# A hybrid diffusion block on one core: rotated queries' low part laid out over 128 rows, and another order of the two arms of the expert branch

## The chip, the cores and the metric

The kernel runs on one core of one Trainium2 chip. The metric is the time of one execution on the device in microseconds (us); the runs of a kernel are compared by their median. The engines are named as in the profile: PE is TensorE (PEld its weight loads), DVE is VectorE, ACT is ScalarE, POOL is GpSimd, and SP is SyncE, which issues the transfers of the weights. A letter q behind a name (PEldq, SPq) is the engine's sequencer.

## What is computed

Two layers act on 256 latent tokens and 256 context tokens of 1024 features. Each layer normalizes and modulates the tokens, projects them, runs three groups of heads side by side, projects back and adds; then comes a dense SwiGLU in layer 0 and a top-2-of-8 expert SwiGLU in layer 1, for latents only. Cut to what the change touches:

```python
qb = apply_rope(qb.reshape(b, n, 2 * DIFF_HEADS, HEAD_DIM), cos, sin)     # differential heads: rotated
na = neighbourhood_attention(qa, ka, va, ka_c, va_c, rpb)                 # neighbourhood heads: not rotated
s = einsum('bqhd,bkhd->bhqk', q, k) * HEAD_DIM ** -0.5                    # HEAD_DIM = 64
p = softmax(s); a = p[:, :, 0] - lam * p[:, :, 1]                         # two softmaxes per differential head
top_vals, top_idx = top_k(h @ w_router, 2)                                # how many latents an expert has depends on data
y = sum over e of gates[e] * (silu(h @ w1[e]) * (h @ w3[e])) @ w2[e]
```

## The kernel before

Tokens stay on chip with features on the partitions. Products are made in float32 from two parts each: a value is split into a rounded high part and the rest, its low part, and `mm3` (L222 to L224) adds high times high, high times low and low times high in one PSUM bank. Weights stream in through SP, are split on ACT (L100) and DVE (L101), and are used once.

**Attention.** A chunk of 128 columns of keys and of queries (`proj_kq`) makes one unit: two neighbourhood units ("na", 0 and 1; not rotated) and four differential ones ("df", 0 to 3; rotated by `rope`). A unit holds two heads or head parts m of 64 features, m = 0 in partitions 0 to 63 and m = 1 in 64 to 127. `key_parts` puts the keys' high part of m into its own half of the tile ks[m] and their low part into the other half; `query_parts` puts the queries' high part into both halves of qs[m], on ACT, and their low part into half m of one tile ql, on DVE (L536). So `scores` needs two products per m: qs[m] with ks[m] over all 128 rows (L560), which gives high times high and high times low, and ql with ks[m] over the 64 rows of half m (L563):

```python
for m in range(2):
    pe.matmul(s[m], qs[m][:, q], ks[m][:, :nk], start=True, stop=False, **kw)
for m in range(2):
    r = slice(64 * m, 64 * m + 64)
    pe.matmul(s[m], ql[r, q], ks[m][r, :nk], start=False, stop=True, **kw)
```

A unit has two query tiles in each group of tokens: layer 0 works on context and latents (256 and 512 keys), layer 1 on latents alone (512 keys). Per query tile the steps are scores, softmax (maximum and weighting on DVE, exponent on ACT), transposes on PE (L580), the split of the transposed block on ACT and DVE (L469, L471), and products with the values (`weigh`).

**Order of the work.** Attention steps wait in a queue with two lanes and are let out between projection products by `pace` (1.3 steps per call in layer 0, 0.4 in layer 1). `finish(keys)` lets out steps until the units named have none left. What order the instructions then get on each engine is decided by a scheduler. `proj_kq` calls finish for the units two before its own. The tiles of the neighbourhood's bias (`hparts["bias"]`, two buffers, loaded by `load_bias`, masked by `mask_bias`) are read when the neighbourhood's scores are finished (L566), and lie idle after that until the next layer.

**The experts.** `route` counts latents per expert and loads one number, few, into a register of every engine (L1300). `first_steps` runs the first part of expert 7, 32 latents wide, with weight tiles loaded ahead. Then `moe_main` branches (L1829): with few above 64 comes `moe_general`, a tree of further branches with a copy of `mix_experts` in each leaf; otherwise one `mix_experts` for two heavy experts and narrow ones for the others. In the program the general arm lies first, some 29,000 rows of PE's, and the arm for few latents behind it, directly ahead of the program's end. With these inputs the arm for few latents is the one that runs. Its weights are read into a ring of twenty tiles of 512 KB (`RAW_M`, L1194) and consumed by narrow products straight from the tile (L1619) and by wide ones after the split (L469, L471). `finish_out` ends the program: two output stores from SP and two from ACT (L1823), and then the engines meet (L1903).

Of the kernel before, what the change touches and what calls it, by code (L numbers as in the profile page):

```python
# [13 lines left out]
F32 = mybir.dt.float32  # L14
F32R = mybir.dt.float32r
# [114 lines left out]
def tile_hybrid_block(ctx: ExitStack, tc: tile.TileContext, x, c, cx, c_ctx, ada_w, ada_b, w_in, w_out, na_rpb,  # L130
                      diff_lambda, diff_subln, conv_w, ffn_w1, ffn_w3, ffn_w2, router_w, moe_w1, moe_w3, moe_w2,
                      final_gain, rope_cos, rope_sin, na_mask, out, dbg=None):
    nc = tc.nc
    sy, act, dve, pe, gp = nc.sync, nc.scalar, nc.vector, nc.tensor, nc.gpsimd
# [39 lines left out]
    hparts = {n: dstack["h"].enter_context(tc.tile_pool(name=n, bufs=1, side="right")) for n in ("hl", "hh", "bias")}  # L174
# [27 lines left out]
    def bank(tag, shape=(128, 512)):  # L202
        t = psum.tile([128, 512], F32, name=tag, tag=tag, bufs=4 if tag == "mm" else 2)
        n = int(np.prod(shape[1:]))
        v = t[:, :n]
        if len(shape) == 3:
            v = v.rearrange("p (a b) -> p a b", a=shape[1])
        return v
# [10 lines left out]
    def mm3(o, ah, al, bh, bl, start, stop):  # L219

        kw = dict(skip_group_check=True)
        return [pe.matmul(o, ah, bh, start=start, stop=False, **kw),  # L222
                pe.matmul(o, ah, bl, start=False, stop=False, **kw),  # L223
                pe.matmul(o, al, bh, start=False, stop=stop, **kw)]  # L224
# [19 lines left out]
    def step(n=1):  # L244
        for _ in range(n):
            for _ in range(2):
                i = turn[0]
                turn[0] ^= 1
                if lanes[i] is None and queue:
                    key, make = queue.popleft()  # L250
                    lanes[i] = key, make(i)
                if lanes[i] is not None:
                    if next(lanes[i][1], "end") == "end":
                        open_work[lanes[i][0]] -= 1
                        lanes[i] = None
                    break
# [3 lines left out]
    def pace():  # L260
        owed[0] += rate[0]
        step(int(owed[0]))
        owed[0] -= int(owed[0])
# [6 lines left out]
    def finish(*keys):  # L270
        while any(open_work.get(k, 0) for k in keys):
            step()
# [137 lines left out]
    st, mo = {}, {}  # L410

    def project(a, b, tags=("mm", "mm")):

        ps = [bank(t, (128, b - a)) for t in tags]
        for u in range(2):
            wh, wl = ws.next()
            wh = wh.rearrange("p (k n) -> p k n", k=4)
            wl = wl.rearrange("p (k n) -> p k n", k=4)
            for k in range(4):
                kt = 4 * u + k  # L420
                for i in range(2):
                    cs = slice(i * 128, (i + 1) * 128)
                    mm3(ps[i], wh[:, k, cs], wl[:, k, cs], hb["h"][:, kt, a:b], hb["l"][:, kt, a:b],
                        kt == 0, kt == KT - 1)
                pace()
        return ps
# [49 lines left out]
    def rope(src):  # L476

        ap = st["apool"]
        t = ap.tile([128, 256], F32, name="rope_t", tag="rope_t", bufs=2)
        u = ap.tile([128, 256], F32, name="rope_u", tag="rope_u", bufs=2)  # L480
        for o, i in ((0, 1), (1, 0), (2, 3), (3, 2)):
            dve.tensor_tensor(out=t[32 * o:32 * o + 32, :], in0=src[32 * i:32 * i + 32, :],
                              in1=sin_t[32 * i:32 * i + 32, :], op=ALU.mult)
        dve.tensor_tensor(out=u, in0=src, in1=cos_t, op=ALU.mult)
        dve.tensor_tensor(out=u, in0=u, in1=t, op=ALU.add)
        return u

    def proj_kq(l, name, rotate, ps=None):

        ap = st["apool"]  # L490
        q0 = 256 * l
        if ps is not None:
            pk, pq = ps
        elif l == 0:
            pk, pq = project(0, 512)
        else:
            ps = [bank("mm"), bank("mm", (128, 256))]
            for u in range(2):
                wh, wl = ws.next()
                wh = wh.rearrange("p (k n) -> p k n", k=4)  # L500
                wl = wl.rearrange("p (k n) -> p k n", k=4)
                for k in range(4):
                    kt = 4 * u + k
                    for i, a in ((0, 0), (1, 256)):
                        cs = slice(i * 128, (i + 1) * 128)
                        mm3(ps[i], wh[:, k, cs], wl[:, k, cs], hb["h"][:, kt, a:], hb["l"][:, kt, a:],
                            kt == 0, kt == KT - 1)
                    pace()
            pk, pq = ps
        units = [("na", 0), ("na", 1)] + [("df", j) for j in range(4)]  # L510
        finish(*units[:max(0, units.index(name) - 2)])

        ks = [ap.tile([128, 512], F32R, name="ks", tag="ks", bufs=6) for _ in range(2)]
        qs = [ap.tile([128, 512 - q0], F32R, name="qs", tag="qs", bufs=6) for _ in range(2)]
        ql = ap.tile([128, 512 - q0], F32R, name="ql", tag="ql", bufs=3)

        def rows_of(v):
            return v.rearrange("p (r n) -> p r n", n=GW)

        def key_parts(src, a):  # L520
            for m in range(2):
                r, o = slice(64 * m, 64 * m + 64), slice(64 - 64 * m, 128 - 64 * m)
                cs = slice(a, a + src.shape[1])
                act.activation(ks[m][r, cs], src[r], AF.Copy)
                dve.tensor_tensor(out=ks[m][o, cs], in0=src[r], in1=ks[m][r, cs].bitcast(F32), op=ALU.subtract)

        def query_parts(src, a):
            src, (hs, low) = rows_of(src), [[rows_of(q[:, a:a + src.shape[1]]) for q in qq] for qq in (qs, [ql])]
            if not rotate:

                src = src[:, :, ::-1]
            for m in range(2):
                r, o = slice(64 * m, 64 * m + 64), slice(64 - 64 * m, 128 - 64 * m)
                for h in (r, o):
                    act.activation(hs[m][h], src[r], AF.Copy, scale=0.125)
                dve.scalar_tensor_tensor(out=low[0][r], in0=src[r], scalar=0.125, in1=hs[m][r].bitcast(F32),  # L536
                                         op0=ALU.mult, op1=ALU.subtract)
        if rotate:
            uk = rope(pk[:, 256:512])
            key_parts(pk[:, :256], 0)  # L540
            uq = rope(pq[:, 256 - q0:512 - q0])
            if l == 0:
                query_parts(pq[:, :256], 0)
            key_parts(uk, 256)
            query_parts(uq, 256 - q0)
        else:
            key_parts(pk, 0)
            query_parts(pq, 0)
        st[name] = (ks, qs, ql)

    def scores(ln, kq, grp, qt, bias=None):

        ks, qs, ql = kq
        nk = 256 if grp == 0 else 512
        q0 = 256 * grp + 128 * qt - st["t0"]
        q = slice(q0, q0 + 128)
        s = [bank(f"at{ln}", (128, nk)) for _ in range(2)]
        kw = dict(skip_group_check=True)
        for m in range(2):
            pe.matmul(s[m], qs[m][:, q], ks[m][:, :nk], start=True, stop=False, **kw)  # L560
        for m in range(2):
            r = slice(64 * m, 64 * m + 64)
            pe.matmul(s[m], ql[r, q], ks[m][r, :nk], start=False, stop=True, **kw)  # L563
        if bias is not None:
            for m in range(2):
                dve.tensor_tensor(out=s[m][:, 256:], in0=s[m][:, 256:], in1=bias[m], op=ALU.add)  # L566
        return s
# [786 lines left out]
    def first_steps():  # L1354

        run = mo["run7"] = light((7,), 32)
        while len(mo["early"]) > TAIL:
            next(run)
            mo["run7_done"] = mo.get("run7_done", 0) + 1
        while mo["folds"]:  # L1360
            mo["folds"].popleft()()
        mo["run7_tasks"] = list(tasks)
        tasks.clear()
        mo["far"].close()
        mo["left"], mo["early"] = mo["early"], {}
# [460 lines left out]
    def moe_main():  # L1826
        route()
        first_steps()
        with tc.If(mo["few"] > 64) as more:  # L1829
            moe_general()  # L1830
        with more.Else():
            mix_experts([0, 1], [((7,), 32), ((2,), 64), ((3, 4, 5), 32)], begun=True)

    def moe_general():
# [18 lines left out]
        with first.Else():  # L1853
# [5 lines left out]
            with many.Else():  # L1859
                mix_experts([0, 1], [((7,), 64), ((2, 3), 64), ((4, 5), 64)])  # L1860

    do(lambda: None, moe_main)

    for add, _ in plan:
# [42 lines left out]
```

## Time and profile before

| what | before |
|---|---|
| median of 3 runs | 1706.23 us (1705.69 to 1714.27) |
| profiled execution | 1709.09 us, span 1707.3 us |
| mean granted PE clock | 0.986 |
| busy: PE, PEld, DVE, ACT, POOL | 96%, 74%, 60%, 37%, 1% |
| moved to and from HBM | 432 MB, 253 GB/s over the span |
| layer 0 attention and projections | about 60 to 265 us |
| layer 0 output and dense SwiGLU | about 265 to 715 us |
| layer 1 attention and projections | about 715 to 860 us |
| routing and first expert steps | about 860 to 914 us |
| the branch | 914 to 921 us |
| experts | 921 to 1695 us |
| final norm and stores | 1695 to 1707 us |

The span runs from the first to the last instruction of the program; 1.8 us of the execution lie around it. A busy PE is modelled, since matmuls overlap: what a matmul costs is better read from start to start in the timeline.

### The profile page before, as it was taken

The page shows a single profiled execution, that of the slowest core. Times are in us where ns is not written, and L with a number is a line of the kernel's source. Part 1 is how long each engine was busy: PE and PEld are TensorE (multiplying, and loading weights), DVE is VectorE, ACT ScalarE, POOL GpSimd, SP SyncE. Part 2 cuts the span into 40 slices and gives each one's busy share as a digit, 9 for nine tenths or more (in the row PEclk, how much of TensorE's full clock was granted, in tenths as well). Part 3 has the DMA queues.
Part 4 walks back from the last instruction along what each step waited for, and adds up shares of the span by engine and source line. Part 5 has one row for each costly group of instructions (what it writes and reads, how often), then busy time and mean ns, then how long its engine had stood idle before and what let it go on. Part 6 is the DMA issues. An engine that isn't in the chain of part 4 may idle for free. (4 is left out here: it accounts for less than half of the span.)

```text
span 1707.3 us, 28490 instructions
## 1 busy us (share of the span) xinstructions
PE 1639.5 (96%) x10942; PEld 1265.7 (74%) x10942; DVE 1030.1 (60%) x2043; ACT 639.0 (37%) x1057; POOL 17.6 (1%) x27
## 2 busy tenths in 40 slices
PE   7999999999999999999987999999999999999996
PEld 4777778988878888988772766676787686868773
DVE  4778877888877884788862353124454535354454
ACT  4555444422212232555533322222343234433341
POOL 0101000000000000000010000000000000000000
PEclk9999999999999999999988999999999999999999
DMA  9744343256555453352498999989999999999995
GB/s 287 179 132 111 99 149 99 88 185 197 197 169 171 154 185 111 99 149 75 162 355 312 409 380 340 349 332 401 360 368 398 364 353 364 405 386 350 388 381 193
DMA packets 234193, 434.66 MB, mean 255 GB/s; under 512 B 23496, under 2 KB 142784, under 8 KB 234048
## 3 DMA queue, kind: packets, MB, share of 16 engines
q1 hardware_dynamic: 232560, 432.14, 71.2%
q8 instruction: 88, 1.44, 0.3%
q10 hardware_dynamic: 1488, 0.62, 0.1%
q14 instruction: 57, 0.47, 0.1%
HBM read 431.66 MB, written 1.05 MB: 253 GB/s over the span
## 5 line engine op out<-in xcount | busy, mean ns | idle before, releaser
L471 DVE TENSOR_TENSOR wlo<-raw,whi 128x1024 fp32r<-128x1024 f32 x168 | 202.9, 1223 | 234.2 <-ACT whi L469 221.5
L222 PE MATMUL H<-xh,whi 128*128 128x256 f32 x896 | 257.2, 287 | 2.6 <-ACT whi L469 1.8
L224 PE MATMUL H<-xh,wlo 128*128 128x256 f32 x896 | 254.5, 284 | 2.0 <-DVE wlo L471 1.9
L223 PE MATMUL H<-xl,whi 128*128 128x256 f32 x896 | 254.1, 284 | 0.0
L469 ACT ACTIVATE whi<-raw 128x1024 fp32r<-128x1024 f32 x168 | 174.3, 1054 | 180.4 <-PE H L223 86.3
L222 PE MATMUL mm<-hh,whi 128*128 128x512 f32 (+1 forms) x648 | 230.4, 356 | 2.4 <-ACT hh L469 1.7
L223 PE MATMUL mm<-hl,whi 128*128 128x512 f32 (+1 forms) x648 | 225.8, 349 | 0.0
L224 PE MATMUL mm<-hh,wlo 128*128 128x512 f32 (+1 forms) x648 | 225.7, 349 | 0.0
L100 ACT ACTIVATE whi<-raw 128x1024 fp32r<-128x1024 f32 x130 | 134.3, 1055 | 241.4 <-DMA raw<-in_ffn_w_dram 128.2
L101 DVE TENSOR_TENSOR wlo<-raw,whi 128x1024 fp32r<-128x1024 f32 x130 | 157.0, 1221 | 60.1 <-ACT whi L100 59.3
L222 PEld LDWEIGHTS H<-xh,whi 128*128 128x128 f32 x896 | 172.3, 192 | 20.0 <-issue 9.3
L224 PEld LDWEIGHTS H<-xh,wlo 128*128 128x128 f32 x896 | 172.4, 192 | 3.0 <-DVE wlo L471 3.0
L223 PEld LDWEIGHTS H<-xl,whi 128*128 128x128 f32 x896 | 172.4, 192 | 0.2
L222 PEld LDWEIGHTS mm<-hh,whi 128*128 128x128 f32 x648 | 122.9, 190 | 22.5 <-issue 4.0
L1619 PE MATMUL L<-raw,xT 128*32 128x512 f32 (+1 forms) x896 | 137.2, 597 | 0.3
L224 PEld LDWEIGHTS mm<-hh,wlo 128*128 128x128 f32 x648 | 122.9, 190 | 16.7 <-issue 2.1
L223 PEld LDWEIGHTS mm<-hl,whi 128*128 128x128 f32 x648 | 123.3, 190 | 13.7 <-issue 0.5
L322 DVE SCALAR_TENSOR_TENSOR ada_t<-raw,scol,ada_t 128x256 f32<-128x256 f32 x266 | 116.6, 482 | 2.8
L1632 ACT ACTIVATE s<-L 128x512 f32<-128x512 f32 x70 | 41.8, 597 | 152.6 <-PE L L1619 127.2
L222 PE MATMUL H<-whi,gh 128*128 128x512 f32 x224 | 90.0, 402 | 3.9 <-ACT gh L469 3.1
L1644 DVE STREAM_TRANSPOSE sT<-tg 128x128 f32<-128x128 f32 x56 | 15.5, 308 | 129.4 <-PE tg L1640 129.3
L223 PE MATMUL H<-wlo,gh 128*128 128x512 f32 x224 | 88.8, 396 | 0.9 <-DVE wlo L471 0.9
(312 smaller groups left out, 2754.1 us busy)
## 6 DMA issues: line engine op xcount, KB each, us to landing
raw<-in_moe_w_dram SPq DMA_DIRECT2D x572, 512.0 KB, 8.3
raw<-in_ada_w_dram SPq DMA_DIRECT2D x40, 1024.0 KB, 5.2
raw<-in_ffn_w_dram SPq DMA_DIRECT2D x32, 1024.0 KB, 5.5
raw<-in_w_in_dram SPq DMA_DIRECT2D x12, 1024.0 KB, 5.2
raw<-in_w_in_dram SPq DMA_DIRECT2D x24, 512.0 KB, 5.4
aw<-in_ada_w_dram SPq DMA_DIRECT2D x16, 512.0 KB, 7.4
far<-in_moe_w_dram SPq DMA_DIRECT2D x16, 512.0 KB, 8.3
raw<-in_w_out_dram SPq DMA_DIRECT2D x5, 1024.0 KB, 5.6
```

The source lines that it names most:

```text
L100: self.nc.scalar.activation(hi, r, AF.Copy)
L101: self.nc.vector.tensor_tensor(out=lo, in0=r, in1=hi.bitcast(F32), op=ALU.subtract)
L222: return [pe.matmul(o, ah, bh, start=start, stop=False, **kw), pe.matmul(o, ah, bl, start=False, stop=False, **kw), pe.matmul(o, al, bh, s ...
L223: pe.matmul(o, ah, bl, start=False, stop=False, **kw),
L224: pe.matmul(o, al, bh, start=False, stop=stop, **kw)]
L322: dve.scalar_tensor_tensor(out=t[:, g, :], in0=raw[:, kt, :], scalar=scol[:, kt, g:g + 1], in1=t[:, g, :], op0=ALU.mult, op1=ALU.add)
L469: act.activation(hi, src, AF.Copy, scale=scale)
L471: dve.tensor_tensor(out=lo, in0=src, in1=hi.bitcast(F32), op=ALU.subtract)
L1619: chained(pe.matmul(o[c * n:(c + 1) * n, :], lhs, rhs, start=(k < ng), stop=(k >= nk - ng), tile_position=(0, c * n), skip_group_check=True))
L1632: act.activation(s, a, AF.Copy)
L1644: dve.transpose(out=t, in_=p)
```

## The change

1. For rotated queries ql becomes a pair of tiles of 128 partitions. In ql[m] the half m has the low part, as before, and the other half is filled with zeros by POOL. Unit 2 takes two tiles of the pool for ql; units 0, 1 and 3 take a buffer of the bias. So that the buffer is free, finish is called for na 0, na 1 and df 0 ahead of them.
2. The second score product of a rotated unit takes ql[m] and ks[m] over all 128 rows. For the neighbourhood it stays at 64.
3. The branch asks for its other side, the arm for few latents, as the one that is reached by falling through.

```diff
-        ql = ap.tile([128, 512 - q0], F32R, name="ql", tag="ql", bufs=3)
+        if not rotate:
+            ql = ap.tile([128, 512 - q0], F32R, name="ql", tag="ql", bufs=3)
+        else:
+            j = int(name[1])
+            if j == 2:
+                ql = [ap.tile([128, 512 - q0], F32R, name="ql", tag="ql", bufs=3) for _ in range(2)]
+            else:
+                finish(*([("na", j)] if j < 2 else [("df", 0)]))
+                t = hparts["bias"].tile([128, 2, 512], F32R, name="bias", tag="bias", bufs=2)
+                ql = [t[:, m, :512 - q0] for m in range(2)]
+            for m in range(2):
+                gp.memset(ql[m][64 - 64 * m:128 - 64 * m].bitcast(F32), 0.0)
...
-            src, (hs, low) = rows_of(src), [[rows_of(q[:, a:a + src.shape[1]]) for q in qq] for qq in (qs, [ql])]
+            src, (hs, low) = rows_of(src), [[rows_of(q[:, a:a + src.shape[1]]) for q in qq]
+                                            for qq in (qs, ql if rotate else [ql, ql])]
...
-                dve.scalar_tensor_tensor(out=low[0][r], in0=src[r], scalar=0.125, in1=hs[m][r].bitcast(F32),
+                dve.scalar_tensor_tensor(out=low[m][r], in0=src[r], scalar=0.125, in1=hs[m][r].bitcast(F32),
                                          op0=ALU.mult, op1=ALU.subtract)
...
         for m in range(2):
+            if isinstance(ql, list):
+                pe.matmul(s[m], ql[m][:, q], ks[m][:, :nk], start=False, stop=True, **kw)
+                continue
             r = slice(64 * m, 64 * m + 64)
             pe.matmul(s[m], ql[r, q], ks[m][r, :nk], start=False, stop=True, **kw)
...
-        with tc.If(mo["few"] > 64) as more:
+        with tc.If(mo["few"] > 64, preferred_fallthrough_block=False) as more:
             moe_general()
```

Lines behind the change have numbers that are 17 higher in the changed kernel; L563 becomes L580 for the neighbourhood and L577 for rotated queries, L560 becomes L574, and the transposes' L580 becomes L597. How the instructions stand is shown at three places.

First, PE at the branch (L1829 before, L1846 after; L1619 and L1636 are the narrow expert products; raw and far are weight tiles). Before:

```order
L1619 MATMUL L<-far_8946,x_9166 32x512
L1640 MATMUL tg<-s,fold_101 32x128 x8
L1300 TENSOR_LOAD ints
L1829 COMPARE_AND_BRANCH
L1839 TENSOR_LOAD ints
L1840 COMPARE_AND_BRANCH
L1452 MATMUL tg<-selG,hk 128x128 x16
L1619 MATMUL L<-raw_8661,xs 128x512
```

After:

```order
L1636 MATMUL L<-far_8964,x_9184 32x512
L1657 MATMUL tg<-s,fold_101 32x128 x8
L1317 TENSOR_LOAD ints
L1846 COMPARE_AND_BRANCH
L1636 MATMUL L<-raw_8743,x_9184 32x512
L1636 MATMUL L<-raw_8747,x_9184 32x512
L1636 MATMUL L<-raw_8751,x_9184 32x512
L1636 MATMUL L<-raw_8755,x_9184 32x512
```

Behind the branch there lay the general arm's first rows; now the products of the arm for few latents follow.

Second, ACT at the end of that arm (L1823 and L1840 are the output stores). Before:

```order
L469 ACTIVATE oh<-of 128x512 x2
L1801 ACTIVATE s,sm<-xT 128x512 x4
L1820 ACTIVATE raw_8709<-raw_8709,sm 128x512
L1820 ACTIVATE raw_8713<-raw_8713,sm 128x512
L1823 DMA out_dram<-raw_8709 128x512
L1823 DMA out_dram<-raw_8713 128x512
L1829 UNCONDITIONAL_BRANCH
```

After:

```order
L469 ACTIVATE oh<-of 128x512 x2
L1818 ACTIVATE s,sm<-xT 128x512 x4
L1837 ACTIVATE raw_8727<-raw_8727,sm 128x512
L1837 ACTIVATE raw_8731<-raw_8731,sm 128x512
L1840 DMA out_dram<-raw_8727 128x512
L1840 DMA out_dram<-raw_8731 128x512
L1846 UNCONDITIONAL_BRANCH
L1856 TENSOR_LOAD ints
L1857 COMPARE_AND_BRANCH
```

Before, nothing follows the arm but the program's end; now the general arm's rows stand between its unconditional branch and the end. DVE, SP and PE have the same there.

Third, PE in layer 1 at a neighbourhood unit's transposes of probabilities (flip, p); mm is a bank of the projections, and pth holds the transposed block's high part for the products with the values (vh). Before:

```order
L224 MATMUL mm<-hh,wlo 128x256
L580 MATMUL at_7351<-flip,p 128x128 x4
L222 MATMUL mm<-hh,whi 128x512
L223 MATMUL mm<-hl,whi 128x512
L224 MATMUL mm<-hh,wlo 128x512
L222 MATMUL mm<-hh,whi 128x256
L223 MATMUL mm<-hl,whi 128x256
L224 MATMUL mm<-hh,wlo 128x256
L222 MATMUL mm<-hh,whi 128x512
L223 MATMUL mm<-hl,whi 128x512
L224 MATMUL mm<-hh,wlo 128x512
```

After:

```order
L224 MATMUL mm<-hh,wlo 128x256
L597 MATMUL at_7317<-flip,p 128x128 x4
L222 MATMUL mm<-hh,whi 128x512
L223 MATMUL mm<-hl,whi 128x512
L224 MATMUL mm<-hh,wlo 128x512
L222 MATMUL mm<-hh,whi 128x256
L223 MATMUL mm<-hl,whi 128x256
L224 MATMUL mm<-hh,wlo 128x256
L222 MATMUL mm<-hh,whi 128x512
L222 MATMUL at_7336<-pth,vh 128x256
```

Before, the first product with this block's values stands 30 projection products behind the transposes; now 7 lie between them.

## Rows read from the trace of the kernel before

**Rows 1.** windows: stretch, length, busy PE, PEld, DVE, ACT, POOL; clock, DMA share, GB/s.

```profile
138.00:265.00 127.00, 121.22 (x691) 91.33 (x688) 104.48 (x278) 63.66 (x150) 4.85 (x2) 0.97 0.38 117
775.00:850.00 75.00, 70.44 (x446) 59.49 (x446) 65.24 (x150) 38.79 (x83) 0.00 (x0) 0.95 0.34 115
```

**Rows 2.** waits of PE, 100:265, 715:860, 930:1690: us, times, longest.

```profile
PE at L580 <- DVE p L638: 3.6, 2, 3.0
...
PE at L580 <- DVE p L638: 2.4, 2, 1.3
...
PE H L222 <- ACT gh L469: 3.1, 2, 1.6
```

**Rows 3.** line L563 in 138:265 and 775:850: minimum, median, maximum ns.

```profile
L563 PE MATMUL at<-ks,ql x32: 379/438/792, 138.6 to 263.1; 64*128 64x512 f32 x16, 64*128 64x256 f32 x16
...
L563 PE MATMUL at<-ks,ql x16: 491/493/792, 775.7 to 847.6; 64*128 64x512 f32 x16
```

**Rows 4.** timeline of PE around one L563 alone, layer 0: start us, us.

```profile
192.82 0.47 PE L560 MATMUL at<-ks,qs 128*128 128x512 f32 x1
193.22 0.50 PE L563 MATMUL at<-ks,ql 64*128 64x512 f32 x1
193.65 0.50 PE L223 MATMUL mm<-hl,whi 128*128 128x512 f32 x1
193.98 0.39 PE L224 MATMUL mm<-hh,wlo 128*128 128x512 f32 x1
```

**Rows 5.** timeline of PE around a pair of L563, layer 1.

```profile
787.69 0.63 PE L560 MATMUL at<-ks,qs 128*128 128x512 f32 x2
788.25 0.49 PE L563 MATMUL at<-ks,ql 64*128 64x512 f32 x2
788.67 0.50 PE L222 MATMUL mm<-hh,whi 128*128 128x512 f32 x1
789.01 0.39 PE L223 MATMUL mm<-hl,whi 128*128 128x512 f32 x1
789.24 0.40 PE L224 MATMUL mm<-hh,wlo 128*128 128x512 f32 x1
```

**Rows 6.** timeline of POOL at the start: a fill of 128 elements.

```profile
0.95 0.20 POOL L182 MEMSET flip<- 128x128 f32 x1
```

**Rows 7.** line L1829, the branch: ns, first and last start us.

```profile
L1829 POOLq COMPARE_BRANCH  x1: 45/45/45, 890.7 to 890.7; - x1
...
L1829 POOLq EVENT_SEMAPHORE  x1: 17/17/17, 891.2 to 891.2; - x1
...
L1829 PEldq COMPARE_BRANCH  x1: 6056/6056/6056, 914.9 to 914.9; - x1
```

**Rows 8.** timeline behind the branch: in brackets idle time before, and releaser.

```profile
919.47 2.19 ACT L469 ACTIVATE xh<-xT 128x512 fp32r<-128x512 f32 x4 [5.85 <-DMA raw<-in_moe_w_dram]
921.19 2.74 PE L1619 MATMUL L<-raw,x 128*32 128x512 f32 x9 [7.09 <-ACT xh L469]
921.34 0.60 DVE L1425 TENSOR_SCALAR sel<-iota,rk 128x128 f32<-128x128 f32 x2 [6.46 <-DMA raw<-in_moe_w_dram]
...
925.65 0.44 PE L1437 MATMUL tg<-ident,sel 128*128 128x128 f32 x2
```

**Rows 9.** windows: the stretch behind the branch; columns as in rows 1.

```profile
918.30:925.10 6.80, 3.58 (x13) 0.78 (x16) 3.46 (x8) 2.19 (x4) 0.00 (x0) 0.50 0.49 179
```

**Rows 10.** timeline of PE before the branch: one quad of 16 products.

```profile
902.85 1.90 PE L1619 MATMUL L<-raw,x 128*32 128x512 f32 x16
```

**Rows 11.** issues of weight tiles (line L1194) in 930:1700.

```profile
DMA to landing us min/median/max: 3.2/8.3/11.5
```

**Rows 12.** the end: the last stores in the timeline, and SP on line L1903.

```profile
1702.25 0.83 SPq L1823 DMA_DIRECT2D out_dram<-raw  x2
1702.53 0.97 ACTq L1823 DMA_DIRECT2D out_dram<-raw  x2
...
L1903 SPq DRAIN  x3: 7/7/13, 1706.5 to 1706.9; - x3
```

## Prediction

> **What bounds the kernel now.** I read the busy times by stage first, then the waits of TensorE (PE), and last the timeline at the two places that the change touches. In the two attention stages with rotated queries (138 to 265 us in layer 0, 775 to 850 us in layer 1) PE is busy for 95% and 94% of the time and VectorE (DVE) for 82% and 87% [rows 1]: PE sets the pace, with DVE close behind. What PE waits for there is first of all the softmax (p of L638): 3.6 us in two waits in layer 0, 2.4 us in two in layer 1; in the expert stage its largest wait is 3.1 us, for an activation [rows 2]. So a microsecond of PE work is nearly a microsecond of the kernel, in every stage.
>
> **The score products.** A score bank takes two products per head part m: L560 over 128 rows, then L563 over 64. Of the 72 L563 the 48 of the rotated queries change, 32 in the first window and 16 in the second [rows 3]. Products, columns and weight loads stay the same in number; rows go from 64 to 128.
>
> What a 64-row product costs is read from start to start. Products of 512 columns in a row start 0.23 us apart (789.01 to 789.24 in [rows 5]). Alone: L560 at 192.82, L563 at 193.22, L223 at 193.65, L224 at 193.98 [rows 4], so 1.16 us for three steps that take 0.69 us elsewhere: 0.47 us lost, at entering, at leaving and in the step after. As a pair: from 787.69 two L560, two L563 and one L222 until 789.01 [rows 5], 1.32 us for five steps of 0.23, 1.15 us: 0.17 us lost. So the two products of a pair overlap and share one change of shape, and still a pair is no cheaper than two full products. Counted in the timeline of both windows, 28 of the 48 stand alone and 20 in ten pairs. I price 256 columns like 512, because the loss lies at the change of shape, and take 0.43 for one alone, a little under the example: 28 x 0.43 + 10 x 0.2 = **14 us** of PE time. A 128-row product among 128-row products has none of it.
>
> The Trainium skill (TensorEngine Tiling (Array Packing), Key Properties) says that a change of the tiling mode drains TensorE; rows 4 and 5 agree. The same page (Overview, Theoretical Speedup) speaks against this change: contraction over at most 64 rows packs up to twofold. By that rule alone the ten pairs would lose their overlap, which is rival 4.
>
> Not all 14 us reach the end: with 7 and 5 us less to cover it, DVE would be busy for about 90% of both windows, and PE's waits for the softmax grow. Bounds: nothing given back (14 us), or 10 us given back (4 us left), almost three times the larger row of such waits. I take a third given back, nearer to the first end, since only four such waits stand in both layers [rows 2]: **-9.5 us**.
>
> The zeros are 16 fills on POOL. A fill of 128 elements takes 0.20 us [rows 6], so 512 take 0.8 us at most. POOL has nothing else to do in these windows but two mask products (4.85 us in [rows 1]), and the fills come before the query parts are made. I cost them at nothing; if each were late by its whole length, L577 would wait 16 x 0.8, 13 us in all.
>
> The calls of finish move neighbourhood steps ahead (third place in the order): in layer 1 a transposed block and the first product that uses it stand 7 projection products apart instead of 30. If the split into two parts on ScalarE (ACT) and DVE isn't done by then, PE waits. That is inside the third given back; its bad end is rival 3.
>
> **The branch.** PE's branch lasts 6.06 us; POOL, whose second arm lies near, goes on 0.5 us after its branch began [rows 7]. PE is idle for 7.09 us until 921.19, ACT for 5.85, DVE for 6.46 [rows 8]. The Trainium skill (Runtime: NRT & Kernel Launch, Instruction fetch mechanics) says that a taken branch to code outside what has been fetched waits for a transfer of that code; PE's and POOL's lengths agree. With the short arm directly behind, the branch isn't taken, and I take **6.1 us** off PE. The 0.8 us of the counter's load between 914.1 and the branch at 914.9 stay.
>
> Then the clock: 918.3 to 925.1 us ran at a granted clock of 0.50 (1.2 GHz) [rows 9], after the idle. The quad of 16 expert products behind the branch takes from 921.19 to 925.65, 4.46 us [rows 8]; a quad at full clock took 1.90 us [rows 10]. Without the long idle I expect full clock: **2.5 us** more. The next step on PE needs a DVE row of 0.60 us [rows 8] that now starts near 916, in time. The weights: a tile lands 8.3 us after its issue, at most 11.5 [rows 11]; a ring of twenty is there, and during the pause it filled (DMA share 0.49 in [rows 9]). PE uses up that lead sooner, but what it needs first is loaded. Branch in all **-8.6 us**; bounds -6.1 (the clock falls anyway, or PE waits 2.5 us for a tile) and -9.
>
> **The far jump at the end.** Now the short arm must jump over the general one (second place). No such jump is in this trace: bounds 0.5 us (POOL) and 6.06 us (PE); I take 5.4, nearer to the long end, from ACT's 5.85 us of idle less half a microsecond for the counter's load. PE is done well before. SP issues its last store until 1703.08, ACT until 1703.50, and SP has its landings and checks behind it by 1706.5 [rows 12], so 3.4 us of SP's jump and 3.0 of ACT's are covered. What sticks out is 2.0 to 2.4 us; SP's checks then come after its jump instead of beside the landing, for which I allow 0.3 us: **+2.7 us**; bounds 0 and +3.3.
>
> **Sum.** -9.5 - 8.6 + 2.7 = -15.4 us. The profiled execution took 1709.09 us (span 1707.3, 1.8 around it), 2.9 above the median of the runs, 1706.23; the same difference off the median gives 1690.8, so **1691 us** (-0.9%). About 0.5%, 8.5 us, is what a measurement of this kernel can tell from no change.
>
> **Rivals.**
> (1) DVE and the softmax chain take the attention's gain: its -9.5 shrinks to -3. For it: DVE at 82 and 87% [rows 1]. Against: PE waits little there now [rows 2]. -3 - 5.9 = -8.9: 1697 us. Chance 0.11.
> (2) The branch gains nothing, because one that isn't taken waits for code too, while the end still pays: -9.5 + 2.7 = -6.8: 1699 us. For it: no such branch is in the trace. Against: POOL's 0.5 us [rows 7]. 0.09.
> (3) Slower: in layer 1, where finish packs the neighbourhood steps, PE waits for every softmax. That layer has 12 rounds (6 units of two query tiles); at 3.0 us, the longest such wait seen [rows 2], they are 36 us, less the 2.4 us that are there already: +33.6 - 15.4 = +18: 1724 us. It decides from (15.4 + 2.4) / 12 = 1.5 us a round. Against: two rounds wait now. 0.07.
> (4) Full rows run one after another where pairs overlapped: ten products of 0.23 us more and no loss removed, +2.3 - 5.9 = -3.6: 1703 us. Against: the loss in [rows 5]. 0.03.
>
> **How the numbers follow.** The forecast has 0.70. Its own range: at best -14 - 9 + 0 = -23, 1683 us; at worst -4 - 6.1 + 3.3 = -6.8, 1699 us. To hold 8 in 10 I take in rivals 1 and 2: 1683 to 1702 us, with some room for their own bounds. Faster by over 0.5%: the forecast, half of rival 1 and a third of rival 2, 0.79. Within 0.5%: the rest of these and rival 4, 0.14. Slower: rival 3, 0.07.
>
> **What would show it.** Right: the changed product (L577) among others starts 0.23 us after its neighbour and the next one 0.23 us after it; PE's idle at the branch is about 1 us, and the quad behind it takes about 1.9 us at clock 1.00; 5 to 6 us lie between the last stores of SP and ACT and what follows. By stage: layer 0's attention some 7 us shorter, layer 1's 2 to 3, the branch 8 to 9, the end 2 to 3 longer. Wrong: waits of PE at the transposes that grow by over 5 us, a branch that still lasts 6 us, or a clock of 0.50 in a new place.

## The result and the profile after

| | before | after |
|---|---|---|
| median, runs | 1707.53 us, 4 | 1692.41 us (1690.12 to 1694.52), 4 |
| ratio, 95% interval | | 0.9893 (0.9866 to 0.9919) |
| profiled execution, span | 1709.09, 1707.3 us | 1694.52, 1692.7 us |

By the ratio the changed kernel is 1.07% faster, 18 us of 1709 (14 to 23). By the two medians of the table it is 15.1 us; in the experiments below the medians of the kernel before were a little higher, 1709 to 1711 us. The forecast was -15.4 us and 1691 us, its range 1683 to 1702 us. A second set of six runs (experiment 8) gave 0.9894 (0.9872 to 0.9916).

**The score products.** The same product alone in layer 0 and as a pair in layer 1, in the timeline of PE of the changed kernel (start us, us, ...), against [rows 4] and [rows 5]:

```profile
177.48 0.39 PE L574 MATMUL at<-ks,qs 128*128 128x512 f32 x1
177.71 0.39 PE L577 MATMUL at<-ks,bias 128*128 128x512 f32 x1
177.94 0.39 PE L222 MATMUL mm<-hh,whi 128*128 128x512 f32 x1
178.17 0.39 PE L223 MATMUL mm<-hl,whi 128*128 128x512 f32 x1
...
782.05 0.63 PE L574 MATMUL at<-ks,qs 128*128 128x512 f32 x2
782.51 0.63 PE L577 MATMUL at<-ks,bias 128*128 128x512 f32 x2
782.98 0.39 PE L222 MATMUL mm<-hh,whi 128*128 128x512 f32 x1
783.21 0.40 PE L223 MATMUL mm<-hl,whi 128*128 128x512 f32 x1
```

L574, L577 and L222 alone take 0.69 us from start to start, three times 0.23; in [rows 4] three such steps took 1.16 us. The four products of the pair and L222 take 1.16 us, five times 0.23; in [rows 5] it was 1.32 us. The loss at the change of shape is gone in both.

The windows of PE in the two attention stages (columns as in [rows 1]):

```profile
138.00:253.00 115.00, 109.73 (x660) 86.85 (x661) 96.34 (x268) 59.23 (x142) 1.35 (x2) 0.99 0.43 124
763.00:840.00 77.00, 73.12 (x498) 66.34 (x498) 71.70 (x160) 43.04 (x90) 0.61 (x2) 0.98 0.33 117
```

PE is still busy for 95% of both, DVE now for 84% and 93% instead of 82% and 87%. (The windows are shifted to where the rotated scores now stand; they do not hold the same instructions as those of [rows 1].) The waits of PE in 100 to 265 us and in 265 to 340 us (us, times, longest) of the changed kernel, and, last, the largest one of the kernel before in 265 to 340 us:

```profile
PE at L597 <- DVE p L655: 2.7, 4, 1.7
PE at L574 <- DVE ptl L471: 1.1, 1, 1.1
```
```profile
PE at L673 <- DVE sm L237: 1.8, 1, 1.8
PE at L222 <- ACT pth L469: 1.7, 1, 1.7
```
```profile
PE at L580 <- DVE p L638: 0.5, 1, 0.5
```

Against the kernel before, the wait for p fell from 3.6 us [rows 2] to 2.7, but behind the last scores of layer 0 there are two new ones, for the split of a transposed block (pth) and for the inverse root in a differential head's norm (L673, from DVE's chain in L229 to L237). They are not the price of the fuller rows: experiment 4's kernel, which has the changed kernel's order and 64 rows, has them too. They came with the changed kernel's order of the steps (the calls of finish alone, experiment 3, don't make them); from the last rotated scores to the first SiLU of layer 0's dense part it takes 71 us before, 77 in experiment 4's kernel and 78 in the changed one.

**The branch.** Line L1846, PE's two branches (ns minimum/median/maximum, first and last start), the timeline of PE and ACT behind the first, and the window around it:

```profile
L1846 PEldq COMPARE_BRANCH  x2: 95/1974/3852, 907.2 to 1679.0; - x2
```
```profile
906.51 2.19 ACT L469 ACTIVATE xh<-xT 128x512 fp32r<-128x512 f32 x4 [0.58 <-DMA raw<-in_moe_w_dram]
907.50 1.92 PE L1636 MATMUL L<-raw,x 128*32 128x512 f32 x16 [1.09 <-DMA raw<-in_moe_w_dram]
```
```profile
904.00:925.00 21.00, 16.95 (x182) 7.58 (x178) 9.03 (x23) 9.42 (x18) 0.00 (x0) 1.00 1.04 397
```

PE's branch takes 0.095 us instead of 6.06 [rows 7], PE is idle for 1.09 us instead of 7.09, the quad behind it takes 1.92 us instead of 4.46 [rows 8], at a granted clock of 1.00 instead of 0.50 [rows 9].

**The end.** The waits of SP at the meeting of the engines, before, and SP on lines L1846 and L1920 after ([rows 12]):

```profile
SPq L1903 <- DMA out_dram<-raw: 3.0, 4, 1.1
```
```profile
L1846 SPq COMPARE_BRANCH  x2: 41/47/53, 883.4 to 1687.5; - x2
...
L1920 SPq DRAIN  x3: 7/7/13, 1691.9 to 1692.2; - x3
```

SP's jump begins at 1687.5 us, behind its last store, and its first check starts at 1691.9: 4.4 us in which the jump stands where SP waited for the landing before. Between PE's last product and the span's end lie 12.5 us instead of 11.5.

**By stage.** In the table every profile is cut at the same five places: the first SiLU of layer 0's dense part (L944), the first transpose of the routing (L1261), the first wide expert product (H), PE's last product and the span's end. The numbers are the us between them; the kernels are those of the experiments.

| kernel | start to SiLU (layer 0) | to routing (layer 1) | to first wide product (branch) | to PE's last (experts) | to the end |
|---|---|---|---|---|---|
| before | 334.2 | 544.1 | 55.9 | 761.7 | 11.5 |
| branch alone (1) | 336.3 | 543.9 | 47.2 | 762.4 | 12.5 |
| finish, layer 1 (9) | 336.1 | 539.8 | 59.5 | 764.5 | 11.5 |
| finish alone (3) | 341.1 | 539.8 | 59.3 | 761.4 | 11.5 |
| 64 rows (4) | 336.7 | 539.8 | 45.8 | 762.5 | 12.5 |
| scores alone (2) | 328.4 | 537.6 | 57.1 | 761.5 | 11.5 |
| after | 331.8 | 538.8 | 47.2 | 762.4 | 12.5 |
| after, again (8) | 336.0 | 537.5 | 47.2 | 760.2 | 12.5 |
| no general arm (5) | 331.0 | 537.7 | 48.5 | 761.4 | 11.9 |
| pause (6) | 331.2 | 538.7 | 55.7 | 761.5 | 12.5 |

Five of the kernels have the same instructions up to the routing (experiments 2, 5, 6, 8 and the changed kernel). Among them the first column still differs by up to 7.6 us (328.4 to 336.0), the second by 1.3. So a stage is read from several profiles, never from one pair. Each profile is also one run of its kernel and need not be a typical one: that of experiment 2, 1697.8 us, was the fastest of six (median 1702.2), that of experiment 9, 1713.2 us, the slowest of twelve (median 1709.8).

### The profile page after: what moved, and what is told of

The parts are those of the page before. It is cut to its first block, busy times and chain, and to the rows that moved or that the text cites. A ratio compares the mean times of both kernels' runs of the same rounds, so it can differ in the third digit from the quotient of the medians.

```text
span 1692.7 us, 28524 instructions
## 1 busy us (share of the span) xinstructions
PE 1630.3 (96%) x10942; PEld 1268.0 (75%) x10942; DVE 1026.3 (61%) x2043; ACT 639.4 (38%) x1057; POOL 25.6 (2%) x43
## 5 line engine op out<-in xcount | busy, mean ns | idle before, releaser
L222 PE MATMUL H<-xh,whi 128*128 128x256 f32 x896 | 257.7, 288 | 2.6 <-ACT whi L469 1.8
L222 PE MATMUL mm<-hh,whi 128*128 128x512 f32 (+1 forms) x648 | 230.2, 356 | 1.7 <-ACT t2k L298 1.2
L222 PEld LDWEIGHTS H<-xh,whi 128*128 128x128 f32 x896 | 172.5, 192 | 20.0 <-issue 9.3
L222 PEld LDWEIGHTS mm<-hh,whi 128*128 128x128 f32 x648 | 123.5, 191 | 21.3 <-ACT t2k L298 2.8
L1636 PE MATMUL L<-raw,xT 128*32 128x512 f32 (+1 forms) x896 | 137.2, 597 | 0.3
L224 PEld LDWEIGHTS mm<-hh,wlo 128*128 128x128 f32 x648 | 123.3, 191 | 15.1 <-issue 0.2
L222 PE MATMUL H<-whi,gh 128*128 128x512 f32 x224 | 90.2, 403 | 3.9 <-ACT gh L469 3.1
```

What stands on the lines that cost most here:

```text
L1636: chained(pe.matmul(o[c * n:(c + 1) * n, :], lhs, rhs, start=(k < ng), stop=(k >= nk - ng), tile_position=(0, c * n), skip_group_check=True))
```

## The experiments

Ratios are to the kernel before, run on the same chip (11 to 19 runs, median 1709 to 1711 us); 0.1% is 1.7 us.

**1. The branch alone.** The kernel before with

```diff
-        with tc.If(mo["few"] > 64) as more:
+        with tc.If(mo["few"] > 64, preferred_fallthrough_block=False) as more:
```

> The kernel before with the arm for few latents behind the branch and nothing else. By the two traces the branch gave PE 8.6 us and the end took back 1.0 us, so I expect 7.6 us less than before (ratio 0.9955), with a branch of about 0.1 us on PE, the quad behind it in 1.9 us at clock 1.00, and everything up to the branch as before (routing at 878.3 us). Rival: the gain at the branch needs the earlier arrival that the attention gave, for instance because weights are then further ahead; then PE would wait for tiles behind the branch and less than 5 us would be left.

Measured: 0.9945 (0.9929 to 0.9962), -9.4 us. From the routing to the first wide product it took 47.2 us instead of 55.9, -8.6, and the end 1.0 more. The whole kernel gained somewhat more than these two make, 9.4 against 7.6 us, which lies within the interval (6.5 to 12). The branch's gain needs nothing of the attention.

**2. The scores alone.** The changed kernel with the branch's line as before.

> The changed kernel with the general arm in front again: score products over 128 rows, zeros and calls of finish alone. I expect routing some 7.7 us earlier than before (near 870.6), and from there on the kernel before: a branch of 6 us on PE, a clock of 0.50 behind it. In all 7 to 8 us less than before (ratio 0.9955). If the two parts do not add up (rival: one gives the other its gain), e1 and e2 together differ from 14.6 us by more than 3.

Measured: 0.9955 (0.9943 to 0.9968), -7.7 us. PE's branch is long again:

```profile
L1846 PEldq COMPARE_BRANCH  x1: 6156/6156/6156, 901.3 to 901.3; - x1
```

0.55% and 0.45% make 1.0%, the whole change 1.07%: the two parts add up within their intervals.

**3. The order alone.** The kernel before with the added calls of finish, without the zeros and the fuller rows.

```diff
+        if rotate and int(name[1]) != 2:
+            j = int(name[1])
+            finish(*([("na", j)] if j < 2 else [("df", 0)]))
         ql = ap.tile([128, 512 - q0], F32R, name="ql", tag="ql", bufs=3)
```

> The kernel before with the three added calls of finish and nothing else: 64 rows, no zeros, general arm in front. Theory: the order alone is worth nothing or costs a little: routing at 876 to 882 us, total within 4 us of before. Rival (order makes the gain): routing near 871 and 7 us less than before. Packed neighbourhood steps without cover (the slower rival of the prediction) would show as waits of PE at the transposes in 735 to 775 us, over 5 us in all.

Measured: 1.0017 (1.0005 to 1.0029), +2.9 us. The order doesn't make the gain. By the table it does two things: layer 1 becomes 4.3 us shorter and layer 0 longer, 341.1 us against 334.2 to 336.3. The scores of layer 1 before, and with the added calls:

```profile
718.00:847.00 129.00, 122.93 (x811) 105.66 (x811) 107.27 (x225) 71.30 (x145) 0.00 (x0) 0.97 0.39 123
```
```profile
725.00:850.00 125.00, 121.64 (x815) 104.03 (x813) 107.80 (x227) 71.13 (x145) 0.00 (x0) 1.00 0.40 127
```

The clock is 1.00 instead of 0.97. A 0.50 stretch of 6.8 us that starts at 836 us in the kernel before is gone, which at half speed can cost 3.4 of the 4.3 us. In layer 0 one profile can't tell the added 5 to 7 us from the spread of 7.6 us.

**4. The rows alone.** The changed kernel with every step where it was, and the second product over half the rows.

```diff
-                pe.matmul(s[m], ql[m][:, q], ks[m][:, :nk], start=False, stop=True, **kw)
+                r = slice(64 * m, 64 * m + 64)
+                pe.matmul(s[m], ql[m][r, q], ks[m][r, :nk], start=False, stop=True, **kw)
```

> The changed kernel, but the second score product of rotated units takes only the 64 rows of half m, as before; zeros, finish and the order of every instruction stay as in the changed kernel. Theory (the change of shape costs PE 0.4 us a product): 64-row products are back with some 0.4 us lost at each, about 14 us of PE work, of which part falls into waits that are there already; routing at 876 to 882 us instead of 870.6, the kernel 5 to 11 us slower than the changed one. Rival (the new order of the steps makes the gain, rows cost nothing): routing stays at 870.6 and the time is that of the changed kernel within 2 us.

Measured: 0.9941 (0.9929 to 0.9954), 0.48% above the changed kernel: the rows alone are worth 8 us (some 4 to 12 by the two intervals). The order of the instructions is that of the changed kernel on PE, DVE, ACT and POOL in both attention stages, so nothing but the rows differs. The product of 177.71 us above, in this kernel's timeline:

```profile
180.42 0.39 PE L574 MATMUL at<-ks,qs 128*128 128x512 f32 x1
180.74 0.50 PE L578 MATMUL at<-ks,bias 64*128 64x512 f32 x1
181.16 0.50 PE L222 MATMUL mm<-hh,whi 128*128 128x512 f32 x1
181.51 0.40 PE L223 MATMUL mm<-hl,whi 128*128 128x512 f32 x1
```

1.09 us where full rows take 0.69, 0.40 lost. Over all 43 places with such products, from the start of the neighbour ahead to the second start behind, and less 0.23 us for 512 columns and 0.12 for 256 in each step, this kernel loses 18.7 us, and the profiles of experiments 2 and 8 and of the changed kernel 5.5, 6.1 and 6.7: 12 to 13 us of PE time are saved. The Trainium skill (TensorEngine Tiling (Array Packing), Key Properties) says that a change of the tiling mode drains TensorE; this pair of kernels, with 0.40 us lost at a 64-row product and none at a full one, agrees.

Not all of it reaches the end, and the same pair shows part of why. PE's waits with 64 rows, in 100 to 265 us, in 265 to 340 us (two rows) and in layer 1 (715 to 860 us):

```profile
PE at L598 <- DVE p L656: 1.1, 1, 1.1
```
```profile
PE at L674 <- DVE sm L237: 1.9, 2, 1.8
PE at L222 <- ACT pth L469: 1.5, 1, 1.5
```
```profile
PE at L598 <- DVE p L656: 1.3, 2, 0.9
```

With full rows the waits for p are 2.7 and 1.7 us, so they grow by 2.0 us where the order is held; the two waits of the tail, 1.8 and 1.7 us with full rows, do not. The other 2 to 3 us of what is given back were not found.

**5. No far jump.** The changed kernel with the general arm left out (`moe_general()` replaced by `pass`).

> The changed kernel with the general arm left out (its leaves and branches are not in the program; with these inputs that arm is never run, so the output stays). The jump over it at the end then goes nowhere far. Theory: in the changed kernel's profile the jumps of SP and ACT at the end take 3.8 and 3.9 us, and most of that lies beside the stores' landing; only about 1 us sticks out. So the end's jumps fall below 0.6 us each, and the kernel is 0.5 to 2 us faster than the changed one (ratio to before near 0.988). Rival, the prediction's term: the far jump costs 2.7 us, ratio near 0.9877 or below. Second rival: nothing sticks out, the same ratio as the changed kernel's, 0.9893. By the profile: from SP's last store to SP's last check, shorter by 1 us (theory), 2.7 us (rival) or 0.

Measured: 0.9889 (0.9869 to 0.9908), against 0.9893 and 0.9894 with the arm; 0.7 to 0.9 us, which the intervals do not tell from nothing or from 2.7 us. The profile tells more. PE's branches, and the waits of SP at the end:

```profile
L1846 PEldq COMPARE_BRANCH  x2: 90/135/180, 906.7 to 1677.8; - x2
```
```profile
SPq L1920 <- DMA out_dram<-raw: 2.8, 4, 0.9
```

The jump takes 0.18 us instead of 3.85, and SP waits for the landing again. From PE's last product to the end it takes 11.9 us, against 12.5 with the arm in all its profiles and 11.5 in the four kernels with the branch as before: the far jump costs 0.6 us against the near one, and the near one some 0.4 against none. The difference lies with SP: from the end of its last store to its first check it takes 3.5 us before, 3.8 with the near jump and 4.5 with the far one. The theory's 0.5 to 2 us holds at its lower end, and as a difference to before it is 1.0; the rival's 2.7 us does not hold.

**6. A pause without far code.** The changed kernel with sixteen multiplications by one, on DVE, at the head of the arm.

```diff
+            x7 = mo["rows"].v["x"]
+            for _ in range(16):
+                dve.tensor_scalar(out=x7, in0=x7, scalar1=1.0, scalar2=None, op0=ALU.mult)
```

> The changed kernel with sixteen multiplications by one on DVE, over the latents' rows for the narrow products, put at the head of the arm for few latents: PE has to wait for them, some 6 us, with no far code to be fetched. It tells what lowered the clock behind the branch before. Theory: the idle alone does it; behind the pause a stretch of 3.4 to 6.8 us has a granted clock of 0.50 and the quad of 16 products takes 4 us or more, so the kernel loses the pause and 2 to 2.5 us: 8 to 9 us in all, ratio near 0.9945. Rival: the fall of the clock belongs to the branch's code transfer, or to the place; then the quad takes 1.9 us at full clock and the loss is the pause alone, 6 us, ratio near 0.993. Second rival: a pause is made up by the weights that gather meanwhile, the loss is below 3 us, ratio below 0.991.

Measured: 0.9957 (0.9941 to 0.9973), 0.64% above the changed kernel, 10.9 us; in the table 8.5 us between routing and the first wide product. PE was done with its narrow products at 916.1 us and waited for the first wide one. Its largest wait there, and the window at the lower clock:

```profile
PE H L222 <- ACT whi L469: 9.5, 1, 9.5
```
```profile
919.70:929.90 10.20, 3.87 (x16) 3.57 (x17) 5.28 (x8) 5.54 (x10) 0.00 (x0) 0.50 1.03 408
```

So the clock falls after an idle stretch without any far code: the rival falls. The quad kept its 1.92 us, since it runs ahead of the pause here; the half clock met 4.4 us of wide products instead (925.5 to 929.9), which by the clock costs some 2 us (the table's experts column, 761.5 us against 760.2 to 762.4, is too uneven to show it). The second rival falls too: the weights kept coming meanwhile (DMA share 1.03), and the loss is far above 3 us.

**7. Other rates.** The changed kernel with `RATES = (1.3, 0.4)` set to other values, in search of a kernel that beats both.

> The changed kernel with 1.6 instead of 1.3 attention steps let out per call in layer 0. In the changed kernel PE had won 9 us at the last scores of layer 0 (253.6 against 262.8 us from the start) and had 2.4 us of it left at the dense part's first activation, because the last steps behind the projections wait for the softmax and the splits (3.5 us in two waits) at a granted clock of 0.50. Theory: with steps let out earlier less is left for that tail, 2 to 5 us faster than the changed kernel, ratio 0.9865 to 0.988. Rival: DVE is the bound of that stage by now, so that waits for the softmax grow earlier by as much as the tail loses: the same within 2 us, or slower.

> The changed kernel with 0.55 instead of 0.4 attention steps let out per call in layer 1. There DVE was busy for 92 per cent of 775 to 850 us, and PE's waits stayed small. Theory: layer 1 has no tail that costs, so that a faster rate gains nothing; DVE's queue is denser, 0 to 4 us slower than the changed kernel, ratio 0.989 to 0.992. Rival: the last steps before the routing cost as in layer 0, and letting them out earlier gains 2 us or more, ratio below 0.988.

> The changed kernel with 1.15 instead of 1.3 attention steps let out per call in layer 0; with 1.6 the kernel had become 16 us slower, with waits of PE for the splits and the softmax that grew from 3.6 to 11 us and 13.6 instead of 6.8 us at a clock of 0.50 between 135 and 350 us. Theory: DVE and ACT can't keep up with a faster rate, so that a slower one packs the attention less densely; the waits for p fall, but more steps are left behind the last projection: within 4 us of the changed kernel, ratio 0.987 to 0.992. Rival, the tail decides: each step that is left costs PE a wait there, 5 us or more slower, ratio 0.9925 or more.

> The changed kernel with 0.33 instead of 0.4 attention steps let out per call in layer 1; with 0.55 it had become 6 us slower by the ratios (0.9928 against 0.9893). Theory: layer 1's steps are let out in time by the calls of finish anyway, and DVE is less dense: within 3 us of the changed kernel, ratio 0.9875 to 0.991. Rival: the steps that are left stand in a tail before the output projection with waits of PE, 5 us or more slower, ratio 0.992 or more.

Measured:

| rates | ratio |
|---|---|
| 1.3, 0.4 (changed kernel) | 0.9893 (0.9866 to 0.9919) |
| 1.6, 0.4 | 0.9988 (0.9975 to 1.0001) |
| 1.15, 0.4 | 0.9944 (0.9923 to 0.9966) |
| 1.3, 0.55 | 0.9928 (0.9908 to 0.9947) |
| 1.3, 0.33 | 0.9917 (0.9893 to 0.9940) |

None is faster. For 1.6 the theory fell: the kernel became 16 us slower, and the tail got worse, not better. The rival named a slower kernel too, but by waits for the softmax, and those fell from 2.7 to 1.1 us. For 1.15 the rival held (5 us or more slower). For 0.55 the theory's sign held, with a little more than the 4 us that it allowed; for 0.33 the figure lies between theory and rival, and its interval reaches the changed kernel's 0.9893. The waits of PE from 135 to 350 us at 1.6:

```profile
PE at L673 <- DVE sm L237: 5.5, 3, 3.3
PE at L222 <- ACT pth L469: 5.5, 3, 3.4
```

At 1.15 one wait of L673 is 5.8 us. (L673 waits for the norm of a head, not for the softmax as the expectations have it.) Layer 0's steps are let out neither earlier nor later without loss; the tail can't be moved away by the rate. At 1.6 the SiLU comes at 346.1 us instead of 331.8, so most of the loss lies in layer 0. These waits account for some 7 us of it; what else the faster rate costs there stays open.

**8. The changed kernel again.**

> The changed kernel itself, without an edit, in more runs: its ratio so far rests on four (0.9893, 0.9866 to 0.9919), too few to tell 1 us. Theory, end costs 1 us: ratio 0.9892 to 0.9897, that is 0.5 to 1.5 us above the kernel without the general arm (0.9889). Rival, the end costs 2.7 us: 0.990 or more. Second rival, nothing: 0.989 or less. By the profile: the jumps of SP and ACT at the end take 3 to 4 us again, and from SP's last store to the span's end it takes 5.2 to 5.8 us against 5.0 without the arm. And, since the changed kernel stood in layer 0 with a 0.50 stretch at 275 us in one profile: if that belongs to the kernel it is there again, with the first activation of the dense part near 332 us; if it was chance, it is missing and that activation comes 2 us or more earlier.

Measured: 0.9894 (0.9872 to 0.9916). The ratio lies where the theory has it, but its interval holds both rivals. The end takes 12.5 us again and SP's last store stands 5.3 us ahead of the span's end. The 0.50 stretch at 275 us is there again, now 6.8 us long, and the SiLU comes at 336.0 us. But in the profiles of experiments 2, 5 and 6, which have the same instructions up to there, the stretch is missing, and the SiLU comes at 328.4, 331.0 and 331.2 us. So the waits of layer 0's tail belong to the kernel; the stretch at half clock comes and goes from execution to execution.

**9. The order in layer 1 alone.** The edit of experiment 3 under `if l == 1 and ...`.

> The kernel before, with the added calls of finish in layer 1 alone: no fuller rows, no zeros, the branch as before. With the calls in both layers it had been 0.17% slower, but its profile had layer 1's scores in 124.8 us against 129.2 and 128.9 in two profiles without them, and its layer 0 longer. Theory: the order gains some 4 us in layer 1 and loses more than that in layer 0, so that this kernel is 3 to 5 us faster than before, ratio 0.997 to 0.9985, with layer 1's scores in 125 us and the first activation of the dense part at 334 to 337 us. Rival: the 4 us in layer 1 are chance of one execution, and the calls cost or gain nothing there: ratio 0.9995 or more, scores in 128 us or more.

Measured: 0.9995 (0.9982 to 1.0008): the whole kernel goes by the rival, the stages by the theory. Layer 1 is 4.3 us shorter again, and layer 0 as before (336.1 us). In this profile the gain was lost behind the far branch, where it took 59.5 us instead of 55.9 to the first wide product, and among the experts (764.5 us instead of 761.7). It is the slowest of twelve runs, 3.4 us above their median, so it doesn't show how much is lost there in a typical one. The stretch there at the lower clock, in this kernel, and in experiment 2's:

```profile
913.20:930.30 17.10, 10.66 (x46) 2.93 (x50) 4.12 (x11) 3.77 (x7) 0.00 (x0) 0.50 0.69 251
```
```profile
904.60:914.80 10.20, 5.99 (x19) 1.29 (x20) 3.46 (x8) 2.19 (x4) 0.00 (x0) 0.50 0.43 135
```

Before it was 6.8 us [rows 9]. The four profiles with the branch as before have 6.8, 10.2, 17.1 and 17.1 us of it and take 55.9, 57.1, 59.3 and 59.5 us; without a far branch the changed kernel has none and takes 47.2.

## Why the prediction was right, step by step

- **PE sets the pace in the attention:** held. PE stays at 95%, and 8 of the 12 to 13 us saved on PE reach the end (experiment 4). The forecast was 14 us saved and 9.5 that arrive; about a third is given back, as it said, though the third was a choice between wide bounds and the measured share is no sharper (4 to 12 us arrive). The way in which it is given back is in part the forecast's: with the order held, PE's waits for p grow by 2.0 us. The two new waits in layer 0's tail are none of it; they come with the order and stand there with 64 rows too.
- **The zeros:** held. None of the larger waits of PE names POOL; with them and the added order, but without the rows (experiment 4), the ratio is 0.9941, against 0.9945 for the branch alone.
- **The calls of finish:** this step failed in kind, though little in the sum. The prediction put their effect inside the third given back, and its bad end at +18 us. Alone they cost 2.9 us in both layers and nothing measurable in layer 1 alone, but they move time between stages: layer 1 became 4.3 us shorter in all three profiles that have the calls without the fuller rows (the spread there is 1.3 us). In the two of them with calls in layer 0 that layer is 1 to 6 us longer, which its spread of 7.6 us doesn't let two profiles show.
- **The split by stage:** wrong, in layer 1 for that reason. Forecast were 7 us in layer 0 and 2 to 3 in layer 1. By the means of the table layer 0 gained 3.9 us (335.5 in the three kernels with the old scores and order there, 331.7 in the five with the new) and layer 1 6.0 (544.0 in two, 538.1 in five). The rows alone, experiment 4 against the five, are near the forecast: 5.0 and 1.7 us. Together the two layers gained 9.8 us, against 9.5.
- **The branch:** -8.6 us, as worked out, in the profiles of experiment 1 and of the changed kernel. Its two terms, the idle of PE and the clock behind it, are both seen. But the exact match is luck: the profile from which the clock's term was read has the shortest 0.50 stretch of four. The mean of the four profiles with the far branch lies 11.1 us above that of the four with the short arm behind it (experiments 1, 4, 8 and the changed kernel), outside the forecast's bound of 9.
- **The jump at the end:** the term that was mis-sized, +1.0 instead of +2.7 us. I took 5.4 us for a jump from the branch under load; with the weights all loaded PE's took 3.85 us and SP's stretch from jump to check 4.4, of which the 3.5 us from its last store to its first check before cover all but 1. With 4.4 in place of 5.4 us, the forecast's own cover of 3.4 us gives that 1.0; its allowance of 0.3 us for the checks was not needed.
- **The rivals:** DVE takes the gain (1): no; with the order held the waits for p grew by 2.0 us only, and 8 us arrive. The branch not taken waits too (2): no, 0.095 us. Packed neighbourhood steps (3): no; PE waits 1.7 us for p in two waits of layer 1, 2.4 before. No loss at pairs (4): no, 0.23 us a step.
- **The signs:** the changed product, the idle at the branch and the quad behind it came as named. Of the signs of being wrong one came: a clock of 0.50 in a new place, 3.4 us at 275 us in the changed kernel's profile. It is missing in three of the five profiles alike up to there, and its 1.7 us at half speed do not overturn the sum. At the end 4.4 us came instead of the 5 to 6 named.

By stage the sum is -9.8 - 8.6 + 1.0 = -17.4 us, and with the mean of the branch's profiles -9.8 - 11.1 + 1.0 = -19.9 us; the ratio gives 18 us (14 to 23) of 1709, the first medians 15. That the forecast of -15.4 met the last so closely is partly luck: its end term was 1.7 us too dear, and its branch term, read from one profile, up to 2.5 us too small.

## What to carry to other kernels

Read a matmul's price from start to start in the timeline, with its neighbours: a half-height product of 0.23 us cost 0.40 us more among full ones, and a pair of them 0.17. Put the arm that runs while other engines wait directly behind its branch and let the far jump fall where a transfer covers it. Read a term that hangs on the clock from several profiles, not from one. To price one part of a change, hold the order of the instructions and change that part alone: against the kernel before, the waits for p seemed to fall; with the order held they grew. And an edit that only moves steps is to be run alone: it can gain in one stage what it loses in another.

## What was not expected of the hardware

- A jump of PE to far code took 6.06 to 6.16 us at the branch, while weights moved at some 400 GB/s, and 3.3 to 3.9 us at the end, where some 4 GB/s moved (1679 to 1683 us); to near code it took 0.18 (experiment 5). The Trainium skill (Runtime: NRT & Kernel Launch, Instruction fetch mechanics) says that a taken branch to code outside what has been fetched waits for a transfer of it; these numbers agree. Whether the load makes the difference between 6.1 and 3.9 us was not tried.
- The same idle of 7.1 us at the far branch was followed by 6.8 to 17.1 us at the lower clock, with 3.6 us between the best and the worst of four profiles. What sets the length stays open.
- The same instructions up to the first SiLU took between 328.4 and 336.0 us in five profiles. The stretches at a clock of 0.50 differ between them, and so do some waits of PE in layer 0's tail: for pth 2.7 us in the slowest, 1.3 in the fastest.
